# Moving the matrices of a decoder trunk to 512-byte multiples of on-chip memory

## The chip, the cores and the metric

The kernel runs on one core of a Trainium2 chip. The metric is the device time of one execution in microseconds (us). On-chip memory (SBUF) has 128 partitions; a tile takes the same bytes in each of its partitions, so its address is a number of bytes from a partition's start. TensorE reads two operands of every matmul from there: the stationary one, which is loaded into the array first (LDWEIGHTS, engine row PEld in the profile), and the moving one, which is streamed through it (MATMUL, row PE). Products are summed in banks of PSUM.

## What is computed

A decoder trunk of two layers on one sequence of 256 tokens and width 1024. A layer is: RMS norm, one input projection, three groups of mixers side by side (retention, sparse attention, chunked gMLP), an output projection with a residual sum, then RMS norm, a SwiGLU feed-forward of width 2816, and a residual sum.

```python
def reference(x, attn_norm, w_in, w_out, ...):
    for l in range(DEPTH):                       # 2
        h = rms_norm(x, attn_norm[l])
        proj = h @ w_in[l]
        r_q, r_k, r_v, r_g, n_q, n_kv, n_g, gm_z = jnp.split(proj, split_points, axis=-1)
        ...                                      # retention, nsa, spatial_gating
        mix = jnp.concatenate([ret_o, nsa_o, gm_o], axis=-1)
        x = x + mix @ w_out[l]
        h = rms_norm(x, ffn_norm[l])
        gate, up = jnp.split(h @ w_gate_up[l], 2, axis=-1)
        x = x + (jax.nn.silu(gate) * up) @ w_down[l]
    return x
```

## The kernel before

All is float32. A large product is made of three: each operand is split into a high part that TensorE takes at full rate (type float32r) and the low rest, and high x high, high x low and low x high are summed in one PSUM bank.

**Weights** come as a stream of pieces of [128, up to 1024] in the order of their use (`PIECES`). A piece is loaded into one of three staging tiles `wst` (at the start also into slices of the tile `PT`, which is not yet in use), ScalarE copies it to a tile `whi`, VectorE writes the rest `wst - whi` to a tile `wlo`; there are six of each (`stream_load`, `stream_hi`, `stream_lo`).

**Products.** `project` multiplies with the activations as the stationary operand (`hcat`, of which `hh` and `hl` are the halves) and the weights as the moving one, 512 columns wide in most chunks; it serves the seven chunks of the input projection and the first chunk of the feed-forward. `project_t` serves the other ten chunks of the feed-forward: there the weights are stationary and `hcat` moves, for each 128 rows of weights four matmuls of 512 columns (high and low activations in one) and four of 256. `residual` serves the output and the down projection: the stationary operand is what the mixers or the feed-forward left (`gmh`/`gml`, `nsh`/`nsl`, `rth`/`rtl` for 8 blocks of 128 rows; `ah`/`al` for 22), the moving one the weights, for two halves of the tokens and two halves of the 1024 columns. The first and last few blocks are done half by half, those between for all four parts in turn; in the last layer the fourth part is two of 256 columns (acc and sm banks).

**Order.** A small scheduler in the kernel (`Desk`) writes the order of all instructions while the program is built: threads (`fork`) hand it operations with estimated durations, and it picks by priority and estimated time. The estimates know shapes and engines, not addresses.

**Addresses.** Tiles that live through the whole program are taken one after the other from a pool `keep` (`fixed`); each takes its bytes, rounded up to 32. The first one begins at byte 16512 of a partition, behind what the system and some constants hold. Small tiles of a few numbers are taken when they are first asked for (`tiny`), behind the others. On top of them a pool of the layer's mixers (`mix_open`) and then, in the same place, one of its feed-forward (`ah`, `al`, `rbc`) is opened.

From the sizes follows where the matrices begin, as the rest of their address in multiples of 512: `wst`, `whi`, `wlo`, the scratch tiles `w2k` and `w1k`, `x`, `hcat` and `cst` 128; `B`, `wsT`, `w1` 416; the pools of a layer begin at 150304, so `gmh`, `gml`, `nsh`, `nsl`, `rth`, `rtl`, `Q`, `Kh`, `Kl`, `aT` and all `ah` and `al` 288; `V`, `PT` and all that stands behind `aT` (2176 bytes) 416.

Of the kernel before, what the change touches and what calls it, by code (L numbers as in the profile page):

```python
# [10 lines left out]
F32R = mybir.dt.float32r  # L11
I32 = mybir.dt.int32
AF = mybir.ActivationFunctionType
# [138 lines left out]

START = [(0, 0), (1, 0), "w", "w", (0, 1), (1, 1), "w", "w"]

NR, NREP = 33, 3
# [13 lines left out]
class Op:  # L171
    def __init__(self, engine, call, dur, table, lat, prio, banks):
        self.engine, self.call, self.dur, self.table = engine, call, dur, table
        self.lat, self.prio, self.banks = lat, prio, banks
# [221 lines left out]
class Trunk:  # L396
    def __init__(self, ctx, tc, x, wts, cst, oh, relb, par, w1, w2, wsT, out):
        self.ctx, self.tc, self.nc = ctx, tc, tc.nc
        nc = self.nc
        self.d = dict(x=x, wts=wts, cst=cst, oh=oh, relb=relb, par=par, w1=w1, w2=w2, wsT=wsT, out=out)  # L400
        self.PE, self.V = Engine("PE", nc.tensor), Engine("DVE", nc.vector)
        self.A, self.G = Engine("ACT", nc.scalar), Engine("POOL", nc.gpsimd)
        self.SP, self.GQ = Engine("DMA", nc.sync), Engine("SWDMA", nc.gpsimd)

        def preload(table):
            if table == "lnexp":
                nc.scalar.preload_act_table_set("natural_log_exp_and_others")

        self.desk = Desk(preload)
        self.keep = ctx.enter_context(tc.tile_pool(name="keep", bufs=1))  # L410
        psum = ctx.enter_context(tc.tile_pool(name="psum", bufs=1, space=bass.MemoryType.PSUM))
        bank = lambda n: psum.tile([128, 512], F32, tag=n, name=n)
        self.acc = Pool([bank(f"acc{i}") for i in range(4)])
        self.sm = Pool([bank(f"sm{i}") for i in range(4)])
        self.norms = 0
        self.wst = Pool([self.fixed(f"wst{i}", [128, 1024]) for i in range(3)])
        self.whi = Pool([self.fixed(f"whi{i}", [128, 1024], F32R) for i in range(6)])
        self.wlo = Pool([self.fixed(f"wlo{i}", [128, 1024], F32R) for i in range(6)])
        self.w2k = Pool([self.fixed(f"w2k{i}", [128, 512]) for i in range(6)])
        self.w1k = Pool([self.fixed(f"w1k{i}", [128, 256]) for i in range(4)])  # L420
        self.x = [self.fixed(f"x{t}", [128, D]) for t in range(2)]
        self.hx = self.fixed("hcat", [128, KD, 2, T], F32R)
        self.hh, self.hl = self.hx[:, :, 0, :], self.hx[:, :, 1, :]
        self.tinies = {}
        n = L * len(PIECES)
        self.loaded = [Event() for _ in range(n)]
        self.split_hi = [Event() for _ in range(n)]
        self.ready = [Event() for _ in range(n)]
        self.hi, self.lo, self.st = {}, {}, {}
        self.used = 0  # L430
        self.started = False
        self.extra = []

    def fixed(self, name, shape, dt=F32):
        return self.keep.tile(shape, dt, tag=name, name=name)

    def tiny(self, name, shape, dt=F32):
        if name not in self.tinies:
            self.tinies[name] = self.fixed(name, shape, dt)
        return self.tinies[name]  # L440
# [86 lines left out]

    def setup(self):
        nc = self.nc
        c = self.fixed("cst", [128, C_W])  # L530
        self.cst = c
        self.ident = c[:, C_ID : C_ID + 128]
        self.tri = c[:, C_TRI : C_TRI + 128]
        self.rowvalid = c[:, C_RV : C_RV + 1]
        self.vmask = c[:96, C_VM : C_VM + 6]
        self.dec = c[:, C_DEC:].rearrange("p (h n) -> p h n", h=6)
        self.kc = self.fixed("kc", [128, 2, 2, 16], F32R)
        self.B = self.fixed("B", [128, 6, 256])
        self.Bc = self.fixed("Bc", [128, 2, 3, 2, 16])
        self.par = self.fixed("par", [128, P_W])  # L540
        self.qg = self.fixed("qg", [128, 1])
        self.wsT = self.fixed("wsT", [128, 4, 128])
        self.w1 = self.fixed("w1", [128, 2, 16, 64])
        self.w2 = self.fixed("w2", [128, 64])
        self.ev_cst, self.ev_bias, self.ev_scr = Event(), Event(), Event()
        self.ev_par = [Event() for _ in range(L)]
        self.ev_lay = [Event() for _ in range(L)]
        self.ev_cmp = [Event() for _ in range(L)]
        self.ev_dec = Event()
        self.ev_w = [Event() for s in START if s == "w"]  # L550
        self.ev_sent = [Event() for s in START if s == "w"]
        self.ev_x = [[Event(), Event()] for _ in range(2)]
# [16 lines left out]
    def load_start(self):  # L569
# [5 lines left out]
        i = 0  # L575
        for step in START:
            if step == "w":
# [434 lines left out]
    def compress(self, l):  # L1012
        PE, V, A, G, give, tiny = self.PE, self.V, self.A, self.G, self.desk.give, self.tiny
# [42 lines left out]

        pk = yield Need(self.sm)
        yield PE.matmul(pk[:32, :64], hk, self.w2[:64, :], start=True, stop=True)
        sq, ss = tiny("csq", [32, 64]), tiny("css", [32, 1])
        yield A.activation(sq, pk[:32, :64], AF.Square, accum_out=ss)  # L1060
        yield V.tensor_scalar(ss, ss, 1.0 / 64, EPS, op0=ALU.mult, op1=ALU.add)
        r = yield from self.rsqrt(ss, "crs")
        kd = tiny("kd", [32, 2, 64])
        yield [V.tensor_scalar_mul(kd[:, i, :], pk[:32, :64], r) for i in range(2)]
        give(self.sm, pk)
        pt = yield Need(self.sm)
# [319 lines left out]
    def mix_open(self, l):  # L1386
        pool = self.tc.tile_pool(name=f"mix{l}", bufs=1, reuse_waits="tile")
        mix = pool.__enter__()

        def tl(name, shape, dt=F32):  # L1390
            return mix.tile(shape, dt, tag=name, name=f"{name}_{l}")

        self.gmh, self.gml = tl("gmh", [128, 2, 256], F32R), tl("gml", [128, 2, 256], F32R)
        self.nsh = [tl(f"nsh{j}", [128, 256], F32R) for j in range(3)]
        self.nsl = [tl(f"nsl{j}", [128, 256], F32R) for j in range(3)]
        self.rth, self.rtl = tl("rth", [128, 3, 256], F32R), tl("rtl", [128, 3, 256], F32R)
        self.Q = tl("Q", [128, 6, 256], F32R)
        self.Kh, self.Kl = (tl(k, [128, 2, 2, 256], F32R) for k in ("Kh", "Kl"))
        self.aT = tl("aT", [128, 2, 272])
        self.Vt = [tl(f"V{t}", [128, 256]) for t in range(2)]  # L1400
        self.PT = tl("PT", [128, 12, 384])
        self.vbd, self.pcT = tl("vbd", [96, 6, 64]), tl("pcT", [96, 256])
        self.rv = [tl(f"rv{t}", [128, 384]) for t in range(2)]
        self.qkT = tl("qkT", [128, 6, 256])
        self.ro = [tl(f"ro{t}", [128, 384]) for t in range(2)]
        self.gmv, self.z = tl("gmv", [128, 512]), {}
        self.S = Pool([tl(f"S{i}", [128, 512]) for i in range(NS)])
        pair = lambda: [Event(), Event()]
        self.ev_gm, self.ev_nq, self.ev_nk, self.ev_v = pair(), pair(), pair(), pair()
        self.ev_gx, self.ev_rq, self.ev_rk, self.ev_ro, self.ev_rt = pair(), pair(), pair(), pair(), pair()  # L1410
        self.ev_tok, self.ev_rv = [pair(), pair()], [pair(), pair()]
        self.ev_ns = [Event() for _ in range(3)]
        self.ev_gate, self.ev_pc = Event(), Event()
        self.ev_u = {(t, h): Event() for t in range(2) for h in range(6)}
        return pool
# [230 lines left out]
    def main(self):  # L1646
# [13 lines left out]
        for l in range(L):  # L1660
# [50 lines left out]
                after = self.store  # L1711
            yield from self.residual(l, idx("down")[0], KF, 3, 4, acted, True, after, l + 1 == L)
            pool.__exit__(None, None, None)


def trunk_kernel(tc, *args):
# [51 lines left out]
```

## Time and profile before

| | us |
|---|---|
| median of 3 runs | 637.78 (637.48 to 637.89) |
| the profiled execution | 638.01 |
| its span, first to last instruction | 636.2 |
| TensorE busy (PE) | 630.5 |
| weight loads (PEld) | 534.7 |
| VectorE busy | 448.5 |
| ScalarE busy | 365.8 |

The profiled execution has 1.8 us around its span. Ends of matmuls are modelled, and matmuls overlap as they stream, so the duration of one says little: what counts is how long after one the next begins. That pace is read from the starts in the timeline, or from a piece of the chain that holds so many matmuls in so many us.

### The profile page before, as it was taken

What the parts mean: (1) busy time and instruction counts of PE and PEld (TensorE: products, weight loads), DVE (VectorE), ACT (ScalarE), POOL (GpSimd) and SP (SyncE); (2) the same over time, 40 slices, a digit from 0 to 9 for tenths busy, and PEclk for the clock granted to TensorE, in tenths of its full rate; (3) what the DMA queues carried; (4) which work ended last, traced back from release to release, by engine and by line L of the source; (5) the groups of instructions that cost most, each with busy time, mean ns of one, the idle gap of its engine ahead of it and who ended that gap; (6) DMA issues with size and microseconds to landing.
All of it is one profiled execution on the core that took longest, in us unless ns stands there. A gap on an engine that the chain in (4) does not pass through costs nothing.

```text
span 636.2 us, 9911 instructions
## 1 busy us (share of the span) xinstructions
PE 630.5 (99%) x3638; PEld 534.7 (84%) x3638; DVE 448.5 (70%) x970; ACT 365.8 (57%) x679; POOL 10.7 (2%) x25
## 2 busy tenths in 40 slices
PE   8999999999999999999999999999999999999997
PEld 6888788888888888888888988888888888888886
DVE  4989996586667767654488898866857767766432
ACT  5869844675555555543377795546755555555330
POOL 1120000000000000100000000000000000000000
PEclk9999999999999999999999999999999999999999
DMA  8974153356555555575436522625565555565631
GB/s 308 305 270 161 31 178 124 114 185 214 187 191 186 183 198 183 189 266 193 133 134 227 176 90 71 203 100 165 189 199 181 193 195 171 191 196 173 201 101 66
DMA packets 33600, 111.63 MB, mean 175 GB/s; under 512 B 4291, under 2 KB 5571, under 8 KB 33552
## 3 DMA queue, kind: packets, MB, share of 16 engines
q1 hardware_dynamic: 33232, 110.62, 52.8%
q8 instruction: 28, 0.46, 0.3%
q0 software_dynamic: 176, 0.36, 0.1%
q14 instruction: 20, 0.16, 0.1%
q10 hardware_dynamic: 144, 0.03, 0.0%
HBM read 109.64 MB, written 1.35 MB: 174 GB/s over the span
## 4 chain that ended last, share of the span: by engine, by line
PE 98%; DMA 1%; DVE 0%; SPq 0%; issue 0%; ACT 0%
PE acc L201 69%; PE sm L201 29%; DMA wst<-in_wts_dram 1%; SPq L201 0%; DVE S L201 0%; DVE x L201 0%; ACT hcat L201 0%; DVE amx L201 0%; ACT whi L201 0%
## 5 line engine op out<-in xcount | busy, mean ns | idle before, releaser
L201 DVE TENSOR_TENSOR wlo<-wst,whi 128x1024 fp32r<-128x1024 f32 (+3 forms) x196 | 234.0, 1197 | 131.6 <-ACT whi L201 130.6
L201 ACT CAST whi<-wst 128x1024 fp32r<-128x1024 f32 (+3 forms) x196 | 200.7, 1028 | 183.7 <-PE sm L201 49.6
L201 PE MATMUL acc<-whi,hcat 128*128 128x512 f32 (+2 forms) x512 | 139.4, 379 | 0.3 <-ACT hcat L201 0.3
L201 PEld LDWEIGHTS acc<-whi,hcat 128*128 128x128 f32 x512 | 91.0, 188 | 15.3 <-ACT whi L201 0.6
L201 PE MATMUL acc<-hcat,whi 128*128 128x512 f32 x320 | 101.2, 396 | 0.0
L201 PE MATMUL sm<-hcat,whi 128*128 128x512 f32 x320 | 99.7, 392 | 0.0
L201 PE MATMUL acc<-wlo,hcat 128*128 128x512 f32 (+2 forms) x256 | 79.5, 378 | 0.0
L201 PEld LDWEIGHTS sm<-hcat,whi 128*128 128x128 f32 x320 | 59.9, 188 | 14.2
L201 PEld LDWEIGHTS acc<-hcat,wlo 128*128 128x128 f32 x320 | 58.8, 188 | 11.8
L201 PE MATMUL sm<-hcat,wlo 128*128 128x256 f32 x320 | 64.0, 281 | 0.0
L201 PE MATMUL acc<-hcat,wlo 128*128 128x256 f32 x320 | 63.8, 281 | 0.0
L201 PEld LDWEIGHTS acc<-hcat,whi 128*128 128x128 f32 x320 | 50.9, 190 | 1.7
L201 PEld LDWEIGHTS acc<-wlo,hcat 128*128 128x128 f32 x256 | 46.4, 188 | 6.9
L201 PE MATMUL acc<-whi,ah 128*128 128x512 f32 (+1 forms) x176 | 50.7, 382 | 0.0
L201 PE MATMUL acc<-whi,al 128*128 128x512 f32 (+1 forms) x176 | 50.6, 381 | 0.0
L201 PE MATMUL acc<-wlo,ah 128*128 128x512 f32 (+1 forms) x176 | 50.4, 380 | 0.0
L201 PEld LDWEIGHTS sm<-hcat,wlo 128*128 128x128 f32 x320 | 49.5, 190 | 0.0
L201 PEld LDWEIGHTS acc<-whi,al 128*128 128x128 f32 x176 | 31.8, 188 | 6.2
L201 PEld LDWEIGHTS acc<-wlo,ah 128*128 128x128 f32 x176 | 31.8, 188 | 6.2
L201 PEld LDWEIGHTS acc<-whi,ah 128*128 128x128 f32 x176 | 31.9, 188 | 6.1
L201 ACT ACTIVATE hcat<-sm,par 128x128 fp32r<-128x128 f32 (+1 forms) x56 | 17.3, 393 | 10.1 <-PE sm L201 9.8
L201 DVE SCALAR_TENSOR_TENSOR hcat<-sm,par,hcat 128x128 fp32r<-128x128 f32 (+1 forms) x56 | 17.4, 362 | 6.0 <-ACT hcat L201 6.0
(213 smaller groups left out, 732.6 us busy)
## 6 DMA issues: line engine op xcount, KB each, us to landing
wst<-in_wts_dram SPq DMA_DIRECT2D x179, 512.0 KB, 3.5
PT<-in_wts_dram SPq DMA_DIRECT2D x7, 512.0 KB, 7.6
wst<-in_wts_dram SPq DMA_DIRECT2D x8, 384.0 KB, 3.1
w<-in_w_dram SPq DMA_DIRECT2D x4, 512.0 KB, 7.7
wst<-in_wts_dram SPq DMA_DIRECT2D x3, 411.0 KB, 4.1
x<-in_x_dram SPq DMA_DIRECT2D x4, 256.0 KB, 5.0
wst<-in_wts_dram SPq DMA_DIRECT2D x4, 256.0 KB, 4.1
B<-scr SPq DMA_DIRECT2D x4, 192.0 KB, 3.7
```

The lines of the kernel that those rows point to most:

```text
L201: return Op(self.name, lambda: fn(*a, **k), dur, table, lat, prio, banks)
```

## The change

Three things are done to addresses, and one to a small tile. A tile `pad` is put in front of the first one, so that `wst0` begins at 16896, a multiple of 512 (`FIRST` is where the pool begins, `SLOT` the rounding, `GRAIN` the multiple). The large tiles of `setup` are taken first and the odd-sized ones (`cst` with 8220 bytes, `par`, `qg`, `w2`) behind them, followed by the small tiles. When the program's last small tile has been taken, a second pad fills `keep` up to a multiple of 512, so that the layer's pools begin at 150528. In these, `aT` goes from the middle to the end. The tile `csq`, into which a square was written for its sum alone, is dropped; the square goes to half of `kd`, which is filled later.

```diff
+FIRST, SLOT, GRAIN = 16512, 32, 512
...
+        self.kept = 0
+
+        self.pad(FIRST)
         self.wst = Pool([self.fixed(f"wst{i}", [128, 1024]) for i in range(3)])
...
     def fixed(self, name, shape, dt=F32):
+        size = 4
+        for n in shape[1:]:
+            size *= n
+        self.kept += -(-size // SLOT) * SLOT
         return self.keep.tile(shape, dt, tag=name, name=name)
+
+    def pad(self, first):
+
+        gap = -(first + self.kept) % GRAIN
+        if gap:
+            self.fixed(f"pad{self.kept}", [128, gap // 4])
...
+        self.B = self.fixed("B", [128, 6, 256])
+        self.wsT = self.fixed("wsT", [128, 4, 128])
+        self.w1 = self.fixed("w1", [128, 2, 16, 64])
+        self.kc = self.fixed("kc", [128, 2, 2, 16], F32R)
+        self.Bc = self.fixed("Bc", [128, 2, 3, 2, 16])
         c = self.fixed("cst", [128, C_W])
...
-        self.kc = self.fixed("kc", [128, 2, 2, 16], F32R)
-        self.B = self.fixed("B", [128, 6, 256])
-        self.Bc = self.fixed("Bc", [128, 2, 3, 2, 16])
         self.par = self.fixed("par", [128, P_W])
         self.qg = self.fixed("qg", [128, 1])
-        self.wsT = self.fixed("wsT", [128, 4, 128])
-        self.w1 = self.fixed("w1", [128, 2, 16, 64])
...
-        sq, ss = tiny("csq", [32, 64]), tiny("css", [32, 1])
-        yield A.activation(sq, pk[:32, :64], AF.Square, accum_out=ss)
+        kd, ss = tiny("kd", [32, 2, 64]), tiny("css", [32, 1])
+        yield A.activation(kd[:, 0, :], pk[:32, :64], AF.Square, accum_out=ss)
...
-        kd = tiny("kd", [32, 2, 64])
...
-        self.aT = tl("aT", [128, 2, 272])
...
         self.S = Pool([tl(f"S{i}", [128, 512]) for i in range(NS)])
+        self.aT = tl("aT", [128, 2, 272])
...
             pool.__exit__(None, None, None)
+        self.pad(FIRST)
```

The residues of all the matrices named above are 0 with it, but for `Bc` (256) and the odd-sized ones.

The order of the instructions is the same on every engine; only names and numbers of tiles differ. On TensorE, at the end of layer 0's down projection and the begin of layer 1's input projection (a `whi`, `wlo` is a piece of weights, the tile behind it the stationary operand), before:

```order
L201 MATMUL acc3_66<-whi4_78,al0_10_1485 128x512
L201 MATMUL acc3_66<-whi5_79,ah0_10_1474 128x512
L201 MATMUL acc3_66<-wlo5_85,ah0_10_1474 128x512
L201 MATMUL acc3_66<-whi5_79,al0_10_1485 128x512
L201 MATMUL acc0_63<-whi0_74,hcat_98 128x512
L201 MATMUL acc1_64<-whi0_74,hcat_98 128x512
L201 MATMUL acc0_63<-wlo0_80,hcat_98 128x512
```

and now:

```order
L203 MATMUL acc3_66<-whi4_79,al0_10_1485 128x512
L203 MATMUL acc3_66<-whi5_80,ah0_10_1474 128x512
L203 MATMUL acc3_66<-wlo5_86,ah0_10_1474 128x512
L203 MATMUL acc3_66<-whi5_80,al0_10_1485 128x512
L203 MATMUL acc0_63<-whi0_75,hcat_99 128x512
L203 MATMUL acc1_64<-whi0_75,hcat_99 128x512
L203 MATMUL acc0_63<-wlo0_81,hcat_99 128x512
```

The tiles' numbers are one higher, since a pad is counted; nothing moved.

On ScalarE, where the square is taken in layer 0, before:

```order
L201 COPY PT_133<-sm_70 128x2x256
L201 ACTIVATE csq,css<-sm_67 32x64
L201 COPY PT_133<-sm_69 128x2x2x128
L201 CAST whi_74<-wst_72 128x768
L201 ACTIVATE crs_z<-css 32x1
```

and now:

```order
L203 COPY PT_133<-sm_70 128x2x256
L203 ACTIVATE kd,css<-sm_67 32x64
L203 COPY PT_133<-sm_69 128x2x2x128
L203 CAST whi_75<-wst_73 128x768
L203 ACTIVATE crs_z<-css 32x1
```

The square writes `kd` instead of `csq`, in the same place. Of the waits three differ: two of VectorE's subtractions into `al` no longer wait for GpSimd, and one of its copies to `aT` now does.

## Rows read from the trace of the kernel before

**Rows 1.** The page: busy time by engine, granted clock by slice, chain by engine.
```profile
PE 630.5 (99%) x3638; PEld 534.7 (84%) x3638; DVE 448.5 (70%) x970; ACT 365.8 (57%) x679; POOL 10.7 (2%) x25
...
PEclk9999999999999999999999999999999999999999
...
PE 98%; DMA 1%; DVE 0%; SPq 0%; issue 0%; ACT 0%
```

**Rows 2.** TensorE's waits: for whom, us in total, times, longest.
```profile
PE sm L201 <- DVE w2k L201: 1.4, 1, 1.4
PE sm L201 <- DMA x<-in_x_dram: 0.5, 1, 0.5
PE acc L201 <- ACT hcat L201: 0.3, 1, 0.3
```

**Rows 3.** The chain in order of time: start us, us, what (matmuls).
```profile
110.28 9.06 PE acc L201 x39
120.23 9.80 PE acc L201 x42
...
259.96 54.37 PE acc L201 x233
...
344.70 9.32 PE acc L201 x41
...
422.55 8.13 PE acc L201 x34
431.57 8.87 PE acc L201 x38
...
621.68 9.84 PE acc L201 x48
```

**Rows 4.** Timeline of TensorE around the end of layer 0: start us, us, operation.
```profile
310.90 0.40 PE L201 MATMUL acc<-whi,ah 128*128 128x512 f32 x1
...
313.00 0.40 PE L201 MATMUL acc<-whi,ah 128*128 128x512 f32 x1
...
322.71 0.62 PE L201 MATMUL acc<-whi,hcat 128*128 128x512 f32 x2
...
324.33 1.07 PE L201 MATMUL acc<-whi,hcat 128*128 128x512 f32 x4
325.24 0.60 PE L201 MATMUL sm<-cst,x 128*128 128x128 f32 x4
```

**Rows 5.** Tile hcat, layer 0's ten chunks: us, busy (count) by engine, PEclk.
```profile
147.00:259.90 112.90, 112.90 (x642) 98.15 (x641) 0.00 (x0) 0.00 (x0) 1.00 0.59 193
```

**Rows 6.** The chain in layer 1's down projection, 600 to 640 us.
```profile
600.13 0.81 PE acc L201 x4
600.95 0.12 PE sm L201
...
620.74 0.81 PE acc L201 x4
```

**Rows 7.** Groups by shape: count, busy us, mean ns, idle time before.
```profile
L201 DVE TENSOR_TENSOR wlo<-wst,whi 128x1024 fp32r<-128x1024 f32 x179 | 219.3, 1228 | 122.0 <-ACT whi L201 121.1 <-issue 0.6
L201 ACT CAST whi<-wst 128x1024 fp32r<-128x1024 f32 x179 | 187.7, 1053 | 173.0 <-PE sm L201 49.6 <-issue 46.1 <-PE acc L201 31.6
...
L201 PE MATMUL acc<-whi,ah 128*128 128x512 f32 x154 | 47.4, 396 | 0.0
...
L201 DVE TENSOR_TENSOR wlo<-PT,whi 128x1024 fp32r<-128x1024 f32 x7 | 8.5, 1220 | 1.2 <-ACT whi L201 1.2
...
L201 PE MATMUL acc<-whi,nsh 128*128 128x512 f32 x24 | 7.5, 395 | 0.0
...
L201 ACT CAST whi<-PT 128x1024 fp32r<-128x1024 f32 x7 | 7.4, 1055 | 0.1
```

**Rows 8.** The chain in the first 30 us: the DMA on it.
```profile
2.10 5.17 DMA wst<-in_wts_dram
```

## The prediction

> **What bounds the kernel now.** I read the page first. TensorE is busy for 99% of the span and the chain that ended last runs through it for 98% [rows 1]. The list of what TensorE waited for confirms that no other engine matters: the three longest entries together are 2.2 us [rows 2]. So the time is the number of matmuls times the pace at which they follow each other, and a change of addresses can only show if it changes that pace. (It could also change VectorE, ScalarE or a DMA, but these are covered; see below.)
>
> So the next view is the chain in order of time, where a piece "PE acc x233" is 233 matmuls with nothing between them, and its length over its count is the pace. Nearly all matmuls of the large products are 512 columns wide. In the down projection of layer 0 the piece of 233 lasts 54.37 us: 233.3 ns each. In the input projection of layer 1 the piece of 41 lasts 9.32 us: 227.3 ns each [rows 3]. [...] Same width, same type, moving operand from the same tiles whi and wlo. 6 ns of 233 is 2.6%, and it wants a reason.
>
> The timeline at the boundary of the layers isolates it [rows 4]. Up to 322.7 us the stationary operand is ah or al; from 322.71 on it is hcat. The order is the same kind on both sides: hi, lo, hi into one bank. From 310.90 to 313.00 us there are nine matmuls in 2.10 us, 233.3 ns each. After the switch to hcat the first seven take 1.62 us (322.71 to 324.33), 231.4 ns each, and the next four 0.91 us (to 325.24), 227.5 ns each. So the slower pace belongs to ah and al as stationary operand, and a run that has just changed needs about seven matmuls to settle.
>
> What differs between hcat and ah is where they lie. The sizes in the code give it: the first tile begins at 16512, 128 past a multiple of 512, and everything up to hcat and cst has sizes that keep this, so wst, whi, wlo, x and hcat begin at residue 128. The constants (8220 bytes) and the small tiles shift the rest: the layer's pool begins at 150304, residue 288. So gmh, gml, nsh, nsl, rth, rtl, Q, Kh, Kl, ah and al are all at 288; behind aT (2176 bytes) everything is at 416. In multiples of 64 bytes that is 0 for hcat and 32 for ah. The pace of 233 goes with 288, the pace of 227 with 128.
>
> **The change part by part.** It puts all of these at residue 0. No instruction is added, dropped or moved on any engine; only csq becomes a part of kd, and aT, B, wsT, w1, kc and Bc change places. I go through what could cost or give time.
>
> *Matmuls whose stationary operand was at 288.* I take it that at residue 0 they run at the pace of hcat, since whi and their stationary tile then begin at the same residue, as whi and hcat do now. The code gives their count: the output projection has 8 x 4 x 3 = 96 of 512 columns per layer, the down projection of layer 0 22 x 4 x 3 = 264, that of layer 1 22 x 3 x 3 = 198, together 654. (Rows 7 show the kinds: 154 for each of three products of ah and al, 24 for each of three of nsh.) By run:
> - The run of 233: 54.37 us now, 233 x 227.3 ns = 52.96 us then: 1.4 us less [rows 3].
> - The four long runs of the output projections (39, 42, 34, 38): 39 x 227.3 ns = 8.86 us against 9.06, 9.55 against 9.80, 8.64 against 8.87; the run of 34 holds another delay (239 ns each), so I give it 34 x 6.0 ns. Together 0.9 us.
> - The last run (621.68 us, 48 matmuls of which 36 are 512 wide): 36 x 6.0 ns = 0.2 us [rows 3].
> - The groups of layer 1's down projection, 15 rows of weights x 3 products, each three matmuls of 512 and two of 256 columns: 22 groups from 600.13 to 620.74 us, 0.937 us each [rows 6]. Here the run never settles. FFN chunks, whose stationary whi is at residue 128 already, show what mixing costs: 642 matmuls in 112.90 us, 1.407 us for four wide and four narrow [rows 5], where four at 227 ns and four of half the width (0.12 us, as in rows 6) would be 1.39: mixing leaves 4 ns per wide matmul on top of the settled pace. So of the 6.0 ns that a settled run saves, the wide ones here save 2 at best: 45 x 3 x 2 ns = 0.3 us. At worst they save nothing; I take 0.15.
> - The remaining 97 (654 - 233 - 153 - 36 - 135) stand in short runs or just behind a break, between 0 and 6.7 ns each; I take 2 ns, 0.2 us.
>
> The sum is 2.85 us. Its ends: all 654 at the settled 226.7 ns (54.37 / 233 less 6.7) give 4.4 us; only the long runs give 2.3.
>
> *The other matmuls* keep equal residues between their two operands (hcat with whi, Kh with Q, PT with V), 128, 288 or 416 before and 0 after. I take zero. [...]
>
> *VectorE and ScalarE.* The split of a weight piece reads the staging tile. From wst (residue 128) it takes 1228 ns on VectorE and 1053 on ScalarE, from PT (residue 416) 1220 and 1055 [rows 7]. A residue is worth under 1% there, and TensorE hides it: zero.
>
> *DMAs.* All are hidden but the first loads, 5.17 us on the chain before the first product [rows 8]. The destinations move, the sources don't. I take zero; a twentieth of it either way would be 0.26 us.
>
> *Waits.* With aT behind S, outside what the FFN tiles cover, two subtractions on VectorE lose a wait for GpSimd and one copy to aT gains one; all of them are for work that ended a layer earlier. The square into kd replaces the one into csq, and the later writes of kd already wait for its sum. Zero; the cover is that none is among TensorE's waits [rows 2].
>
> **The sum.** The profiled execution took 638.0 us, 0.2 above the median of 637.8. 637.8 - 2.9 = 634.9 us, with 633.4 and 635.5 as the ends of this case.
>
> **The rivals.**
> *Nothing moves* (637.8 us). The pace would then not hang on the residue but on something else that ah and hcat differ in, for example that ah lies some 50 KB higher, or that it is written just before. For it: the run with hcat also shows 231 when disturbed, so 227 is a state that a run must reach. Against: gmh, nsh, rth, ah and al are different tiles written by different code, and their long runs (232.3 and 233.3 in the output projection) agree, while hcat does not. [...]
>
> [...]
>
> *Slower* (about 640.9 us). Residue 128 may be what makes hcat fast, and 0 as bad as 288. Then the 576 wide matmuls of the projections go from about 229.3 (between the 227.3 and the 231.4 of rows 3 and 4) to 233.3, 2.3 us, the 640 wide ones of the FFN from about 232 (a quarter of 1.407 us less four times 0.12), 0.8 us, and ah gains nothing: 637.8 + 3.1 = 640.9. If ah gains its 2.9 us all the same, the balance tips once those 1216 lose over 2.4 ns each. Against: with equal residues on both sides nothing else in the rows separates 0 from 128.
>
> **How the numbers follow.** The forecast case gets 0.60, nothing 0.20, more 0.12, slower 0.08. The forecast is 634.9 us. The likeliest case and the one of no change hold 0.80, so the range is 632.8 (the 4.4 us, the DMA's 0.26 and a little of the third case) to 638.2. A change under 0.2% (1.3 us) can't be told from none. Some of the forecast case (0.02) and of the slower one would fall within it: faster 0.70, the same 0.22, slower 0.08.
>
> **What would show it.** Right: in the chain after, the long run of the down projection at about 227 ns (52.9 us for 233), the boundary at layer 1 without a change of pace, FFN chunks still 112.9 us, VectorE's 1228 and ScalarE's 1053 ns as before. [...]

## The result and the profile after

The changed kernel takes 634.46 us (median of 4 runs, 634.43 to 634.87) against 637.84 (637.48 to 638.22), a ratio of 0.9948 with a 95% interval of 0.9931 to 0.9966. The forecast was 634.9. Five more runs of the same kernel, made beside e6, gave 635.18 against 637.67 (0.9957, 0.9944 to 0.9969; e7_after below).

The page after shows the bound unchanged, as in [rows 1]: TensorE at 99%, the chain through it, the granted clock at 0.9 or more of the full one in every slice (1.00 on the mean).

```profile
PE 628.1 (99%) x3638; PEld 534.7 (84%) x3638; DVE 448.0 (71%) x970; ACT 366.0 (58%) x679; POOL 9.9 (2%) x25
...
PEclk9999999999999999999999999999999999999999
...
PE 97%; DVE 1%; DMA 1%; ACT 0%; issue 0%; ACTq 0%
```

So the matmuls are as many as before and follow each other faster. Where, the chain in order of time says (start us, us, what), to be held against [rows 3]:

```profile
109.98 8.87 PE acc L203 x39
...
259.44 52.82 PE acc L203 x233
...
342.57 9.34 PE acc L203 x41
...
420.34 7.94 PE acc L203 x34
429.17 8.65 PE acc L203 x38
...
618.76 9.64 PE acc L203 x48
```

Every run whose stationary operand lay at 288 is shorter: 54.37 to 52.82 (226.7 ns each), 9.06 to 8.87, 8.13 to 7.94, 8.87 to 8.65, 9.84 to 9.64. The run of 41, whose stationary operand is hcat, has not moved (9.32 and 9.34).

The timeline of TensorE at the layers' boundary (start us, us, operation) no longer has the step of [rows 4]:

```profile
309.83 0.39 PE L203 MATMUL acc<-wlo,ah 128*128 128x512 f32 x1
...
311.87 0.40 PE L203 MATMUL acc<-wlo,ah 128*128 128x512 f32 x1
...
318.73 0.60 PE L203 MATMUL sm<-cst,x 128*128 128x128 f32 x4
...
320.56 0.62 PE L203 MATMUL acc<-whi,hcat 128*128 128x512 f32 x2
...
322.17 1.07 PE L203 MATMUL acc<-whi,hcat 128*128 128x512 f32 x4
323.08 0.60 PE L203 MATMUL sm<-cst,x 128*128 128x128 f32 x4
```

From 309.83 to 311.87 nine matmuls take 2.04 us, 226.7 ns each, with ah and al as stationary operand. With hcat the last four take 0.91 us (322.17 to 323.08), 227.5 each, as before. The first seven with hcat still take 1.61 us (320.56 to 322.17), 230.0 each, though ah and hcat now agree. So what unsettles them is not the change of operand alone, as the prediction read [rows 4]: four transposes (318.73) break the run shortly before the switch, and another four stood there in the kernel before (320.88).

The FFN's up projections are as they were. This view and [rows 5] cover one stretch each (112.80 us here, 112.90 there) and show that matmuls with hcat fill it, 642 of them in each; columns as there:

```profile
146.60:259.40 112.80, 112.80 (x642) 98.06 (x640) 0.00 (x0) 0.00 (x0) 1.00 0.59 193
```

The lengths are thus no measurement. The starts in the traces are: from the first to the last of layer 0's 640 up projections it is 112.30 us before and after.

So are the other engines' large groups ([rows 7]: 1228 and 1053 ns):

```profile
L203 DVE TENSOR_TENSOR wlo<-wst,whi 128x1024 fp32r<-128x1024 f32 x179 | 219.4, 1229 | 120.7 <-ACT whi L203 119.6 <-issue 0.6
L203 ACT CAST whi<-wst 128x1024 fp32r<-128x1024 f32 x179 | 188.0, 1053 | 171.7 <-PE sm L203 54.0 <-issue 42.6 <-DMA wst<-in_wts_dram 32.0
```

And the mixed groups of layer 1's down projection go from 0.937 us ([rows 6]) to 0.933: in the chain 22 groups in the 20.53 us from the first of these rows to the last.

```profile
597.30 0.82 PE acc L203 x4
598.11 0.12 PE sm L203
...
617.83 0.82 PE acc L203 x4
```

The narrow matmuls of these groups, 256 float32r columns, take 0.12 us. What the section on the kernel before calls full rate has its measure beside them: the eight float32 matmuls of 256 columns at the kernel's start (`w2k`, 128x256, from 1.44 us on) begin 0.427 us after each other, but for a first step of 0.59, before and after the change.

One piece of this profile was not foreseen. The chain of waits leaves TensorE at the end of layer 0's output projection:

```profile
123.53 4.61 DMA wst<-in_wts_dram
...
129.30 1.23 DVE wlo L203
130.53 0.61 DVE x L203
131.14 0.04 issue
131.18 0.66 PE sm L203 x4
```

A weight piece lands late, its split on VectorE stands ahead of a residual sum, and four transposes wait for that sum: 0.2 us in which TensorE stands still. It does not belong to every execution: the profile of e7_after, the same kernel, has no such gap (its run of 42 there takes 9.56 us, and the transposes follow at once). The chains of e6 and s2 below have a piece like it in layer 1's output projection, the other profiles have none; whether a faster TensorE makes it more likely is open.

### The profile page after: what moved, and what is told of

Its sections match the earlier page's. It is cut to its first block, busy times and chain, and to the rows that moved or that the text cites. A ratio compares the mean times of both kernels' runs of the same rounds, so it can differ in the third digit from the quotient of the medians.

```text
span 633.1 us, 9910 instructions
## 1 busy us (share of the span) xinstructions
PE 628.1 (99%) x3638; PEld 534.7 (84%) x3638; DVE 448.0 (71%) x970; ACT 366.0 (58%) x679; POOL 9.9 (2%) x25
## 4 chain that ended last, share of the span: by engine, by line
PE 97%; DVE 1%; DMA 1%; ACT 0%; issue 0%; ACTq 0%
PE acc L203 67%; PE sm L203 31%; DMA wst<-in_wts_dram 1%; DVE wlo L203 0%; ACT whi L203 0%; DVE x L203 0%; DVE S L203 0%; DVE w2k L203 0%; DVE rtl L203 0%; DVE amx L203 0%; ACT rth L203 0%; ACTq L203 0%
## 5 line engine op out<-in xcount | busy, mean ns | idle before, releaser
L203 PEld LDWEIGHTS sm<-hcat,whi 128*128 128x128 f32 x320 | 59.9, 188 | 14.2
L203 ACT ACTIVATE S<-S,amx 128x256 f32<-128x256 f32 (+1 forms) x48 | 21.2, 454 | 0.6 <-DVE amx L203 0.6
```

Of the source, the lines that this page charges most:

```text
L203: return Op(self.name, lambda: fn(*a, **k), dur, table, lat, prio, banks)
```

## The experiments

Four theories were held against each other. **A:** the stationary operand is fast where a row of it begins at a multiple of 64 bytes, whatever the other does (288 is 32 past one, 128 and 0 are not). **B:** the distance between the stationary and the moving operand counts, not where either lies; this is what the prediction's step on the stationary operands used ("then begin at the same residue"). **C:** multiples of 512 are wanted. **D:** not the residues but the new order of the tiles and its waits.

### e1_pool64: only the layers' pools, moved by 32 bytes

At the end of `main` of the kernel before:

```diff
+        self.fixed("padx", [128, 8])
```

> The kernel before with one unused 32-byte tile behind the small tiles: the layers' pools begin at 150336 in place of 150304, so gmh, nsh, rth, Q, Kh, ah and al are at residue 320 of 512 (a multiple of 64, not of 128), everything else is where it was, whi at 128. Theory A (what counts is where a row of the stationary operand begins within 64 bytes): the run of 233 in the down projection takes 52.8 us (226.7 ns each) in place of 54.4, and the time is that of the changed kernel, 634.5, or a little less since aT stays where it was. Theory B (the two operands have to begin at the same residue of 512) and theory C (multiples of 512 are wanted): the run stays at 54.4 us and the time at 637.8. Theory D (the order of the tiles and the waits do it, not the residues): 637.8 too, with the run at 54.4.

634.54 us, ratio 0.9943 (0.9926 to 0.996). The chain:

```profile
259.38 53.34 PE acc L201 x233
...
343.05 9.33 PE acc L201 x41
...
618.46 9.60 PE acc L201 x48
```

The time is what A expected, but by chance; the run is not: 228.9 ns each, neither A's 226.7 nor the 233.3 of B and C as they stood. D is wrong: no tile changed its order and the gain is there. That the time is whole all the same comes from elsewhere in the same profile, the mixed groups of layer 1:

```profile
597.45 0.80 PE acc L201 x4
598.25 0.11 PE sm L201
598.36 0.80 PE acc L201 x4
```

0.91 us each (0.9136 from the starts of all), where the changed kernel has 0.933. The distance of the operands is 320 - 128 = 192 here.

### e2_pool32 and e3_all32: the pools alone, or everything, at residue 32

e2, at the end of `main` of the changed kernel behind its pad; e3, its constant:

```diff
         self.pad(FIRST)
+        self.fixed("padx", [128, 8])
```
```diff
-FIRST, SLOT, GRAIN = 16512, 32, 512
+FIRST, SLOT, GRAIN = 16480, 32, 512
```

> The changed kernel with one unused 32-byte tile more ahead of the layers' pools: all of a layer's tiles at residue 32, wst, whi, wlo, x and hcat stay at 0. Theory A: the run of 233 is back at 54.4 us, the run of 41 with hcat stays at 9.3 us, and the time is 634.5 + 2.9 = 637.4. Theory B: the same, as the operands no longer agree. Theory C, if any residue but 0 is worse: the same. Theory D: the run stays at 52.8 us and the time at 634.5.

> The changed kernel with its first tile and all of its matrices 32 bytes higher: every residue is 32 in place of 0, so both operands of each matmul still agree. Theory A: the run of 233 takes 54.4 us, the run of 41 with hcat 9.5 to 9.6 us in place of 9.32, the up projections of the FFN (642 matmuls in 112.8 us) slow down too; 634.5 + 2.9 for the output and down projections, + 2.3 for 576 wide matmuls with hcat at 4 ns each, + 0.8 or more for 640 with whi: 640 to 642 us. Theory B: nothing moves, 634.5, run at 52.8. Theory C: as A. Theory D: 634.5.

e2: 637.40 us (ratio 0.9987, 0.9977 to 0.9996), the run of 233 at 54.37. The gain is gone with 32 bytes. e3: 635.88 us (0.9962, 0.9947 to 0.9976), and

```profile
259.62 52.82 PE acc L203 x233
...
342.71 9.32 PE acc L203 x41
```

Both at 32, and both are fast. This ends A and C (they had 640 to 642 us) and speaks for B: the same stationary residue of 32 is slow beside a moving one of 0 and fast beside one of 32. The median lies 1.4 us over 634.5: four runs took 634.93 to 635.16 us and four 636.61 to 637.02. None of the longer four was profiled, so what makes them longer is not shown; the profiled one, at 635.16, spans 633.4 us against the 633.1 of the changed kernel, and what it has more stands before the first run (14.54 against 14.08 us).

### e4_order: the new order with the old residues

```diff
-        self.pad(FIRST)
         self.wst = Pool([self.fixed(f"wst{i}", [128, 1024]) for i in range(3)])
...
-        self.pad(FIRST)
+        self.pad(FIRST - 288)
```

> The changed kernel with the residues of before: no tile ahead of the first (wst, whi, hcat at 128), the pad ahead of the pools chosen so that they begin at 150304 again (residue 288, 32 past a multiple of 64); what the change moved (csq within kd, aT behind S, B, wsT, w1, kc, Bc ahead of the constants) stays moved. Theories A, B and C: the run of 233 at 54.4 us and 637.8 us, or some 0.2 above or below if the move of aT alone is worth something. Theory D: 634.5, run at 52.8.

637.69 us, ratio 0.9993 (0.9982 to 1.0004), the run of 233 at 54.37. The moves of aT, B, w1 and the rest are worth nothing.

### e5_w32: whi and wlo 32 bytes away from everything

```diff
+        self.fixed("padw", [128, 8])
         self.whi = Pool([self.fixed(f"whi{i}", [128, 1024], F32R) for i in range(6)])
         self.wlo = Pool([self.fixed(f"wlo{i}", [128, 1024], F32R) for i in range(6)])
+        self.fixed("padv", [128, 8])
```

> The changed kernel with an unused 32-byte tile ahead of whi and another behind wlo: whi and wlo at residue 32, x, hcat and what follows at 64, the layers' tiles at 0 as before. No stationary operand but whi (in the up projections of the FFN) has left a multiple of 64; all products of whi or wlo now have operands 32 apart. Theory A: 634.5 + 0.8 or more for the FFN's up projections. Theory B: the down and output projections lose 2.9, the input projections with hcat (576 wide matmuls) go from about 229 to 233 ns, 2.3, and the up projections lose 0.8 or more: 640 to 641, slower than the kernel before, and the run of 41 with hcat takes 9.55 us in place of 9.32.

639.72 us, slower than the kernel before (ratio 1.0025, 1.0015 to 1.0035), though ah, hcat and their like all lie at multiples of 64.

```profile
33.20 9.56 PE acc L203 x41
...
261.12 54.37 PE acc L203 x233
...
346.32 9.56 PE acc L203 x41
```

The runs are as B expects, but for one term: the up projections (whi is stationary there, 32 from hcat) lose nothing, with 112.2 us from the first start to the last in each layer where e7_after has 112.3. 634.5 + 2.9 + 2.3 is 639.7, and it meets the time more closely than its parts do: the profiled spans differ by 5.3 us (638.0 and 632.7 in e7_after), of which 0.4 stand ahead of the first run (14.43 against 14.00), so the losses are 4.9.

### s1_scan, s2_scan, s3_scan: which distances

The chunks of ah and al in layer 0 at a residue each, whi and wlo at 0:

```diff
+            off = SCAN if l == 0 else [0] * NCH
+            at = lambda n, c: ffn.tile([128, 640], F32R, tag=f"{n}{c}", name=f"{n}{l}_{c}")[
+                :, off[c] // 4 : off[c] // 4 + 512
+            ].rearrange("p (j n) -> p j n", j=2)
-            ah = [ffn.tile([128, 2, 256], F32R, tag=f"ah{c}", name=f"ah{l}_{c}") for c in range(NCH)]
+            ah = [at("ah", c) for c in range(NCH)]
...
```

> The changed kernel, with ah and al of layer 0 in larger tiles, so that chunk c begins at a residue of its own: 0, 32, 64, 96, 128, 192, 256, 320, 384, 448 and 480 for c = 0 to 10; whi and wlo stay at 0, layer 1 too. Each chunk is the stationary operand of 24 wide matmuls in a row, so the run of 233 becomes a scan of the distance between the two operands. Theory B (after the third and first run: the distance of the stationary from the moving operand counts, not where either lies): 226.7 ns at 0, 233 at 32, 96 and 480, 228.9 at 192 as in the first run; between 226.7 and 229 at the other multiples of 64. If only an equal residue is good, 229 or more at all of them; if the distance counts by multiples of 128 or 256, those are at 226.7. Theory A (the stationary operand's own residue by 64), which the third run has contradicted, would have 226.7 at every multiple of 64.

> The same scan with 0, 4, 8, 16, 24, 48, 56, 40, 160, 224 and 0 for chunks 0 to 10. Theory B with a unit of 64 bytes: everything that is no multiple of 64 is at 233, 4 bytes as much as 32. With a unit of 32: 16 and 48 near 226.7 to 229. If the cost grows with the distance: 4 and 8 lie between 226.7 and 233. 160 repeats the distance of the kernel before (233.3).

> The scan again, at distances just below a multiple of 256: 0, 252, 248, 240, 232, 216, 208, 200, 184, 176 and 0 for chunks 0 to 10. Theory B: the distance counts modulo 256 (0 and 256 gave 226.7 ns, 64 and 320 233.3, 192 and 448 about 229), and 0 is the best; then all of these lie between 228 and 234. If the good place is a range that ends at a multiple of 256, 240 to 252 are at 226.7 or below, and a kernel faster than the changed one would be in reach; 4 and 8 on the other side of 0 gave 232.6 and 230.4.

The times of these single runs (637.78, 635.95, 635.64 us) are not compared; s1 began its first product 1.2 to 2 us later than the other profiles. The timeline of s1, the first row of chunks 2 to 7 (six rows of four matmuls each chunk):

```profile
272.14 1.10 PE L204 MATMUL acc<-whi,ah 128*128 128x512 f32 x4
...
277.74 1.09 PE L204 MATMUL acc<-whi,ah 128*128 128x512 f32 x4
...
283.35 1.10 PE L204 MATMUL acc<-whi,ah 128*128 128x512 f32 x4
...
288.95 1.08 PE L204 MATMUL acc<-whi,ah 128*128 128x512 f32 x4
...
294.45 1.08 PE L204 MATMUL acc<-whi,ah 128*128 128x512 f32 x4
...
299.90 0.40 PE L204 MATMUL acc<-whi,ah 128*128 128x512 f32 x1
```

Each difference over 24 is the pace: 233.3 ns at distance 64, 233.8 at 96, 233.3 at 128, 229.2 at 192, 227.1 at 256 (226.6 once settled). All distances, from the starts of a chunk's last twelve matmuls, the step to the next chunk left out (176, 224, 448 and 480 from shorter stretches):

| pace, ns | at distances |
|---|---|
| 226.6 to 226.7 | 0, 252, 256 |
| 228 to 231 | 8, 24, 176, 192, 200, 240, 448 |
| 231 to 232.8 | 4, 184, 216, 232, 384 |
| 233 to 234 | 16, 32, 40, 48, 56, 64, 96, 128, 160, 208, 224, 248, 320, 480 |

Of 29 distances three are fast, and none is faster than the equal residue. 256, 320 and 448 do what 0, 64 and 192 do, even in the order of their single steps (at 64 and 320 alike 236, 231, 236, 230 ns); 384 gives 231.7 where 128 gives 233.3, so a period of 256 bytes is not the whole rule. There is no unit of 64 or 32, and no gentle slope either: 4 bytes on one side cost 6 ns, 4 on the other nothing. So s1's idea of at most 229 ns at every multiple of 64 falls (64, 128, 320), s2's of a cost growing with the distance, and s3's of a good range at 240 to 252 too; s3's other one, that all of them lie between 228 and 234, falls with 252 (226.7).

### s4_al128: whose stationary operand

```diff
             ah = [ffn.tile([128, 2, 256], F32R, tag=f"ah{c}", name=f"ah{l}_{c}") for c in range(NCH)]
+            ffn.tile([128, 32], F32, tag="padl", name=f"padl{l}")
             al = [ffn.tile([128, 2, 256], F32R, tag=f"al{c}", name=f"al{l}_{c}") for c in range(NCH)]
```

> The changed kernel with an unused tile of 128 bytes between the ah and the al tiles: ah stays at distance 0 of whi and wlo, al comes to 128 (233.3 ns in the scan). In each row of weights twelve matmuls follow: four of ah with whi, four of ah with wlo, four of al with whi. Theory B in the form that a matmul is slowed by its own two operands: the four of al are slow, 9 to 12. In the form that it is slowed by the stationary operand that is loaded for the next matmul while it runs: 8 to 11, the last of wlo is slow and the last of al fast. Both: a third of 233 matmuls at 6.7 ns more, the run at 53.3 us in place of 52.8, and about 635.4 us. If only the mean over a row counts, or other bits of the address, all twelve move alike.

635.84 us (one run), the run of 233 at 53.72. In 14 of the 15 rows of weights that go through all four parts (the first still settles) the twelve starts stand apart, in every row alike, by 231, 226, 227, 227, then 226, 227, 227, 232, then 241, 233, 230, 233 ns. That is 2760 ns a row, where four matmuls at 6.7 ns more make 2747, so the run is 0.4 us longer than the 53.3 expected. The timeline (a window that cuts the row of wlo before its fourth matmul):

```profile
274.51 0.40 PE L203 MATMUL acc<-wlo,ah 128*128 128x512 f32 x1
274.74 1.10 PE L203 MATMUL acc<-whi,al 128*128 128x512 f32 x4
```

The eighth matmul, at 274.51, has the same two operands' residues as the seventh and sixth; all that differs is the stationary operand that is loaded while it runs, al at 128. It takes 232 ns to the next start where they take 227. That load begins with it (274.51 on PEld). So where the next matmul's stationary operand lies bears on the pace of the running one, 232 ns with al at distance 128 against 227 with ah at 0. By the records the load is not the one that lasts longer: in the long runs of the kernel before and of e7_after a load of ah or al takes 187 or 188 ns alike, and PEld is 534.7 us on the pages before and after. How the load acts on the running matmul, no run shows. That the first is at 231, with its own operands and the next load at distance 0, shows that a slowed run does not come back at once. The twelfth (next is ah again) is at 233 either for the same reason or because a matmul's own distance counts as well; the twelve numbers do not tell these apart.

### e6_pool128 and e7_after: the smallest change that makes all distances 0

The kernel before with one tile more, beside the changed kernel:

```diff
+        self.fixed("padx", [128, 88])
```

> The kernel before with one unused tile of 352 bytes behind the small tiles: the layers' pools begin at 150656, residue 128, as wst, whi, wlo, x and hcat do. Nothing is moved to a multiple of 512 and no tile changes its place in the order. Theory B: distance 0 for all products, the run of 233 at 52.8 us, and the changed kernel's 634.5 us, or up to 0.2 less if a part of what the change lost at the end of layer 0's output projection comes from the moved aT. If multiples of 512 count for anything: above 634.5.

> The changed kernel again, beside the run before it: 634.5 us.

634.51 us, ratio 0.9951 (0.9937 to 0.9964), beside 635.18 for the changed kernel (0.9957, 0.9944 to 0.9969), which can't be told apart. The run of 233 is at 52.82 in both. One unused tile of 352 bytes does all that the change does, with every operand at 128.

### e8_d192: two places at distance 192

What e1 showed of the mixed groups, in the changed kernel: ah and al of layer 1, and hcat while it serves the FFN.

```diff
+        self.hbuf = self.fixed("hcat", [128, KD * 2 * T + 16], F32R)
+        self.hcat_at(0)
...
+            if l:
+                ffn.tile([128, 48], F32, tag="padl", name=f"padl{l}")
             ah = [ffn.tile([128, 2, 256], F32R, tag=f"ah{c}", name=f"ah{l}_{c}") for c in range(NCH)]
...
     def to_norm(self, gcol, ev_par):
+        self.hcat_at(16 if gcol == P_G2 else 0)
...
+    def hcat_at(self, c):
+        self.hx = self.hbuf[:, c : c + KD * 2 * T].rearrange("p (k r n) -> p k r n", k=KD, r=2)
+        self.hh, self.hl = self.hx[:, :, 0, :], self.hx[:, :, 1, :]
```

> The changed kernel with distance 192 (the best one in the first experiment for groups that mix widths: 913.6 ns for three wide and two narrow matmuls, 933.3 at distances 0, 32 and 224) in two places: ah and al of layer 1 lie 192 bytes further on, and while hcat serves the FFN it is written and read 64 bytes further on, so that whi, the stationary operand of the up projections, is at -64, that is 192 by 256, from it. The price: in the FFN's first chunk of each layer hcat is the stationary operand at 64, where the scan had 233 ns, so the run of 47 takes 10.95 us in place of 10.69 and its like in layer 0 about as much more, 0.5 in all. Layer 1's down projection: 45 groups by 19.6 ns, 0.85 less (49.45 us from the run of 20 to the run of 48 in place of 50.30). If theory B with timing inside a mixed group decides, the up projections gain about as much per group of four wide and four narrow, 80 x 20 ns = 1.6 us (111.2 us in place of 112.8 per layer): 632.5 us in all. If the up projections don't care, as at distances 0 and 224 (112.80 us both): 634.1.

631.39 us (630.88 to 631.97), ratio 0.9902 (0.9885 to 0.9918): some 3 us below the changed kernel. The chain of e8:

```profile
119.73 9.56 PE acc L203 x42
...
257.96 52.83 PE acc L203 x233
...
427.52 8.65 PE acc L203 x38
...
565.72 4.48 PE acc L203 x20
...
615.20 9.60 PE acc L203 x48
```

And the chain of e7_after, the changed kernel:

```profile
119.64 9.56 PE acc L203 x42
...
259.07 52.82 PE acc L203 x233
...
428.73 8.65 PE acc L203 x38
...
568.03 4.42 PE acc L203 x20
...
618.33 9.64 PE acc L203 x48
```

From the start of the run of 42 to that of the run of 233 lie the FFN's first chunk and layer 0's up projections: 138.23 us against 139.43. Layer 1's lie between the runs of 38 and 20: 138.20 against 139.30. The starts in the traces divide the 2.3 us. The 640 up projections take 110.90 us (layer 1: 110.92) from the first to the last in place of 112.30, a gain of 1.4 us in each layer; the 48 matmuls of the first chunk take 11.83 and 11.84 in place of 11.64, a price of 0.2 us in each where 0.25 was expected. A settled group of four wide and four narrow matmuls goes from 1402 to 1383 ns, on the mean of eight: nearly the 20 ns expected. The expectation's 632.5 us counts the gain of 80 groups, 1.6 us, for one layer only; with both it would have been 630.9, and 631.39 was measured. Layer 1's down projection gains 0.8 (49.48 against 50.30), as expected. The run of 47 that the expectation names belongs to the input projection of layer 1 and not to the FFN; it stays at 10.69.

## Why the prediction was right

Against the profile of e7_after, which has no gap at 131 us (span 632.7, before 636.2), in us:

| step | predicted | measured |
|---|---|---|
| run of 233 | -1.4 | -1.55 |
| runs of 39, 42, 34, 38 | -0.9 | -0.19 - 0.24 - 0.19 - 0.22 = -0.84 |
| run of 48 | -0.2 | -0.20 |
| 45 mixed groups | -0.15 | 45 x 3.6 ns = -0.16 |
| the other 97 matmuls | -0.2 | -0.4, with all that is not listed |
| start to the run of 36 | 0 | -0.37 (14.00 against 14.37) |

**The operands' distance.** Its step was that ah and its like reach hcat's pace because both operands then begin at the same residue. e3, e5 and e6 show that just this counts (52.82, 54.37 and 52.82 us for the run of 233). The remark beside it, 0 and 32 in multiples of 64, was no rule: s1 has 233.3 ns at 64 and 128. The size of the first term is a little more than predicted because 227.3, read from the short run of 41, still holds its first, unsettled matmuls. That a change of the stationary operand by itself unsettles a run for seven matmuls was a misreading: in the changed kernel the seven with hcat still take 230.0 ns each, though no residue changes there. No term of the sum hangs on it.

**All other matmuls at zero.** Right, and for the reason given: their distance stays 0 (runs of 41 and the starts of the up projections unchanged; the up projections alone would not show it, since e5 has them as fast at distance 224). The rival "slower", 0 as bad as 288, is refuted by the same rows, "nothing moves" by e2 and e4 against e6. For the "more" of the chances (0.12, and the third case at the low end of the range) no run shows a ground: of the 29 distances none has a pace below 226.6 ns.

**Mixed groups.** The term is right, the working behind it only half: mixing does not leave a fixed 4 ns on top, and 0.15, the middle of two bounds, was met by luck. At distances 0, 32 and 224 a group takes 933 ns and at 160 937, but at 192 914, and the up projection gains there too (e8: 1383 ns for 1402). I had no row for that.

**DMA, the first loads.** Zero was a choice, and the start moves by more than the quarter of a microsecond allowed for it. In thirteen profiles (all but s1's) the first run begins between 13.93 (e6) and 14.74 us (e2), with 14.08 and 14.00 in two executions of the changed kernel; what stands ahead of it on most chains is the first load of x or of a weight piece, 4.39 to 5.30 us. The six in which the tiles of the first loads lie as in the changed kernel, and e6, are at 14.1 or below, the other six at 14.2 or above, but s1, with the start of the changed kernel address for address, had 5.07 us for that load and began later than any. Whether the addresses have a part in it stays open; no run was made for it alone. Of the 3.5 us by which the two spans differ 3.1 lie behind the start.

**VectorE, ScalarE, waits.** Right: 1229 and 1053 ns, and the longest entry among TensorE's waits is as in [rows 2]:

```profile
PE sm L203 <- DVE w2k L203: 1.4, 1, 1.4
PE sm L203 <- DVE amx L203: 0.2, 1, 0.2
```

e4 shows by itself that the moved tiles cost and bring nothing (637.69 us, 637.89 for the kernel before).

## What to carry to other kernels

Where TensorE is the bound and weights change with every matmul, divide each long run of the chain by its count: two paces for one shape (here 233.3 and 226.7 ns) are a reason to print the addresses of both operands. Begin with equal residues (here 226.7 ns at distances 0 and 256, 232.7 at 4); one unused tile of 352 bytes was enough to get them, and absolute alignment was worth nothing by itself (e6 with all at 128 took 634.51 us, the changed kernel with all at 0 635.18). Where widths alternate, try other distances by experiment and read the effect in the chain's stretches: here 192 was worth another 3 us, as much as the change.

## What the hardware showed that was not expected

- The pace of a matmul of 512 float32r columns with 128 new columns of weights depends on the distance of the two operands in a partition: 226.7 ns at 0, 252 and 256, up to 233.9 elsewhere, and 4 bytes can decide (0: 226.7, 4: 232.7, 8: 230.5, 16: 233.5).
- Where the stationary operand of the next matmul lies counts while the present one still runs (s4: 232 ns for 227, with its own operands unchanged).
- The pattern is exact: the starts of a settled run repeat to the nanosecond over 15 rows of weights, before in a cycle of three matmuls (237, 231, 232), at other distances of two (24: 229, 231) to seven (96). After the change there is no cycle: 226, 227, 227 is one pace of 226.7 in whole nanoseconds.
- The best of the distances tried is another one where wide and narrow matmuls alternate: 192 (914 ns for three wide and two narrow, 1383 for four and four) in place of 0 (933, 1402). Why is open: only 0, 32, 160, 192 and 224 were tried there, and no run shows what takes place inside a group.
